# The mixer's products with h as seven block products, made ahead of the branch products, with the gates kept in DRAM

## The chip, the cores and the metric

The kernel runs on one NeuronCore of a Trainium2 chip. The metric is the device time of one execution in microseconds (us). The engines are TensorE (PE, with its weight loads listed as PEld), VectorE (DVE), ScalarE (ACT), GpSimd (POOL) and SyncE (SP), whose queue issues the DMAs. They run beside each other, each in the order of its own queue, and wait for each other by semaphores. [...]

## What is computed

One layer of a diffusion backbone over 512 latent and 128 context tokens (T = 640), model width 1024, all in float32. The mixer, which the change is about, stands between two SwiGLU blocks (FFN1, FFN2):

```python
z = h @ w_in
q, k, v, g, u, vs, gates = jnp.split(z, IN_SPLITS, axis=-1)
...
r = r.transpose(0, 2, 1, 3).reshape(B, L, RET_V) * g_ret
ret_out = (jax.nn.silu(g) * r) @ w_ret_br
u = jax.nn.gelu(u)
vsf = jax.nn.gelu(vs)
...
sp = jnp.einsum('gij,bnjgc->bnigc', w_sp, vsn) + b_sp.T[:, :, None]
sg_out = (u * sp.reshape(B, L, SG_WIDTH)) @ w_sg_br
gate_r, gate_s = jnp.split(jax.nn.sigmoid(gates), 2, axis=-1)
y = (gate_r * ret_out + gate_s * sg_out) @ w_out
```

In the parts left out, r is the retention per head in both directions, normed, and vsn is the LayerNorm of vsf with g_sg and b_sg. g, u and both gates are four products of the same h with 1024 x 1024 weights; the outputs keep float32 accuracy.

## The kernel before

A float32 matrix is held as two parts, a rounded one (hi) and the rest (lo), and each product is three passes: hi·hi, hi·lo, lo·hi. For h these are the tiles HH and HL, [128, 8, 640]: 8 slices k of 128 features, 640 tokens. Weights come as 512 KB blocks by DMA into `raw`, ACT rounds them to `whi` (L199), and DVE or POOL subtracts to get `wlo` (L206). One list, `steps`, sets in which order the weights are used; `stream` and `flow` prepare them ahead of PE (two steps with `take`, seven with `take7`), five pairs of buffers in a ring. The schedule is written by hand: the program's order is each engine's order.

The mixer runs in these parts. Six groups of token-major products (`group`, matmuls of 512 columns): 0 to 3 give q, k, v of a head each, 4 and 5 give vs, which ACT turns by gelu into VS (the tile F1). Beside them a queue of small tasks, `bg`, works off the heads' retention (`head_tasks`), one task behind every twentieth part of a group; at the end the heads' r stands in F0. Then eight products each of u, gs with sg, g, gr, rt (`one`: 8 k x 3 passes, 384 columns in part A and 256 in part B, 48 matmuls). u stands first, with the LayerNorm of VS beside it: five `ln_step`s for each half of the features, a subtract-and-scale (L1346) and a multiply (L1347) on DVE and an addition on POOL (L1348); then `sp_step` multiplies gelu(u) with the spatial product into Z (tiles ZH, ZL). gs is used at once as sigmoid in the evacuation of sg, the branch product of Z. g gives silu(g)·r, the next Z; gr goes into F0; rt, the branch product, is gated and added, and H takes the sum. Boundary 2 is w_out on H, two norms and the next h; then FFN2.

FFN2 has the form that the change brings to the mixer: `seven` (L781) computes two output blocks over 1024 features as a 2 x 2 block product with seven instead of eight block multiplications (Winograd's scheme). For that the right side needs four sums and differences of the blocks of h, the "forms" (`right_forms`, L654; th, tl in the profile), and each pair of weight blocks four more sums (L161), with seven hi and lo parts of 512 columns (whis, wlos). A block is 4 k x 3 passes of 320 columns, 12 matmuls. Three PSUM banks per pair, X, Y, Z, collect the blocks q0 to q6; X goes on being added to after ACT has copied its state out (p1 after q0, u2 after q2, u3 after q4), so q2, q4 and q5 wait for a copy.

`newton_rsqrt` (L281) makes the reciprocal roots of all norms: three rounds, in each of them two instructions per column of 128 tokens.

## Time and profile before

| | us |
|---|---|
| median of 3 runs (lowest, highest) | 1646.86 (1642.75, 1648.46) |
| the profiled execution | 1649.0 |
| its span in the profile | 1647.2 |
| mean granted clock in it | 0.979 |
| mixer's products, from the end of group 5 to w_out's first matmul | 751.8 to 1099.7 |

The span is the time from the first to the last instruction of one profiled execution. The profiled execution is one run among others; a sum made from its rows is one against its own time, and the runs' median lies 2.1 us lower. Busy time is no measure of what bounds a stage: an engine that is busy 60% of the span can be full in one stage and idle in the next.

### The profile page before, as it was taken

The page shows a single profiled execution, that of the slowest core. Times are in us where ns is not written, and L with a number is a line of the kernel's source. Part 1 is how long each engine was busy: PE and PEld are TensorE (multiplying, and loading weights), DVE is VectorE, ACT ScalarE, POOL GpSimd, SP SyncE. Part 2 cuts the span into 40 slices and gives each one's busy share as a digit, 9 for nine tenths or more (in the row PEclk, how much of TensorE's full clock was granted, in tenths as well). Part 3 has the DMA queues.
Part 4 walks back from the last instruction along what each step waited for, and adds up shares of the span by engine and source line. Part 5 has one row for each costly group of instructions (what it writes and reads, how often), then busy time and mean ns, then how long its engine had stood idle before and what let it go on. Part 6 is the DMA issues. An engine that isn't in the chain of part 4 may idle for free. (4 is left out here: it accounts for less than half of the span.)

```text
span 1647.2 us, 25640 instructions
## 1 busy us (share of the span) xinstructions
PE 1587.5 (96%) x10294; PEld 1540.4 (94%) x10294; DVE 984.7 (60%) x1911; ACT 580.7 (35%) x1083; POOL 489.3 (30%) x304
## 2 busy tenths in 40 slices
PE   8899999999998999999999999999898999999995
PEld 8899999999998788889999999999897999999995
DVE  6768577776757866657621131235848656565656
ACT  4535212222223532332321233224445525344343
POOL 3322112221125322234211111114425434333334
PEclk9899999999998999999999999999899999999997
DMA  9035344443442322212222222233302223122231
GB/s 379 14 122 188 127 146 158 145 171 137 154 141 63 104 65 69 72 58 90 77 102 68 62 77 77 70 133 93 109 27 96 80 75 107 58 81 87 80 116 64
DMA packets 62599, 170.63 MB, mean 104 GB/s; under 512 B 5904, under 2 KB 22544, under 8 KB 62480
## 3 DMA queue, kind: packets, MB, share of 16 engines
q1 hardware_dynamic: 62336, 168.92, 30.7%
q8 instruction: 81, 1.33, 0.3%
q14 instruction: 38, 0.31, 0.1%
q10 hardware_dynamic: 144, 0.07, 0.0%
HBM read 160.05 MB, written 8.91 MB: 103 GB/s over the span
## 5 line engine op out<-in xcount | busy, mean ns | idle before, releaser
L206 POOL TENSOR_TENSOR wlo<-raw,whi 128x1024 fp32r<-128x1024 f32 (+2 forms) x90 | 222.5, 2473 | 754.8 <-ACT whi L199 718.3
L199 ACT CAST whi<-raw 128x1024 fp32r<-128x1024 f32 (+2 forms) x159 | 155.4, 997 | 73.2 <-DMA raw<-in_wout_dram 31.3
L206 POOL TENSOR_TENSOR wlos<-raw,whis 128x512 fp32r<-128x512 f32 (+1 forms) x61 | 83.5, 1371 | 165.3 <-ACT whis L199 133.5
L206 DVE TENSOR_TENSOR wlo<-raw,whi 128x1024 fp32r<-128x1024 f32 (+2 forms) x69 | 90.2, 1308 | 63.4 <-ACT whi L199 62.0
L308 PE MATMUL pBf<-HL,whi 128*128 128x256 f32 x416 | 117.7, 283 | 0.0
L309 PE MATMUL pBf<-HH,wlo 128*128 128x256 f32 x416 | 117.6, 283 | 0.0
L307 PE MATMUL pBf<-HH,whi 128*128 128x256 f32 x416 | 117.6, 283 | 0.0
L416 DVE CUSTOM_DVE_ANT_0 junkc<-wa,cb 128x1024 bf16<-128x1024 f32 x56 | 102.6, 1832 | 1.9
L314 PE MATMUL pg<-whi,HH 128*128 128x512 f32 x240 | 99.4, 414 | 0.0
L199 ACT CAST whis<-raw 128x512 fp32r<-128x512 f32 (+1 forms) x138 | 80.9, 604 | 50.4 <-PE pof213B L309 5.9
L315 PE MATMUL pg<-whi,HL 128*128 128x512 f32 x240 | 95.0, 396 | 0.3 <-DVE HL L384 0.3
L316 PE MATMUL pg<-wlo,HH 128*128 128x512 f32 x240 | 94.4, 393 | 0.0
L308 PEld LDWEIGHTS pBf<-HL,whi 128*128 128x128 f32 x416 | 79.6, 191 | 0.2 <-DVE HL L384 0.2
L309 PEld LDWEIGHTS pBf<-HH,wlo 128*128 128x128 f32 x416 | 79.6, 191 | 0.0
L307 PEld LDWEIGHTS pBf<-HH,whi 128*128 128x128 f32 x416 | 79.5, 191 | 0.0
L411 DVE CUSTOM_DVE_ANT_0 junk<-wa,cb 128x1024 bf16<-128x1024 f32 x58 | 77.1, 1329 | 2.8 <-DMA wa<-in_wada_dram 2.2
L206 DVE TENSOR_TENSOR wlos<-raw,whis 128x512 fp32r<-128x512 f32 (+1 forms) x77 | 66.9, 875 | 9.2 <-ACT whis L199 9.1
L795 PE MATMUL Xf<-th,whis 128*128 128x320 f32 x216 | 67.7, 314 | 2.9 <-ACT p1f L805 1.8
L797 PE MATMUL Xf<-th,wlos 128*128 128x320 f32 x216 | 67.2, 311 | 0.0
L796 PE MATMUL Xf<-tl,whis 128*128 128x320 f32 x216 | 67.2, 311 | 0.0
L316 PEld LDWEIGHTS pg<-wlo,HH 128*128 128x128 f32 x240 | 45.5, 190 | 10.3
L315 PEld LDWEIGHTS pg<-whi,HL 128*128 128x128 f32 x240 | 45.7, 190 | 8.4 <-DVE HL L384 0.6
(2712 smaller groups left out, 5218.5 us busy)
## 6 DMA issues: line engine op xcount, KB each, us to landing
raw<-in_win_dram SPq DMA_DIRECT2D x86, 512.0 KB, 4.4
wa<-in_wada_dram SPq DMA_DIRECT2D x60, 512.0 KB, 3.8
raw<-in_wmix_dram SPq DMA_DIRECT2D x56, 512.0 KB, 3.5
raw<-in_wgrp_dram SPq DMA_DIRECT2D x24, 512.0 KB, 3.6
raw<-in_wout_dram SPq DMA_DIRECT2D x32, 256.0 KB, 2.7
raw<-in_wout_dram SPq DMA_DIRECT2D x16, 384.0 KB, 4.1
st<-in_wada_dram SPq DMA_DIRECT2D x10, 512.0 KB, 10.5
raw<-in_wout_dram SPq DMA_DIRECT2D x16, 320.0 KB, 3.9
```

The lines of the kernel that those rows point to most:

```text
L199: A.copy(hi, parts_[i])
L206: eng.tensor_tensor(lo, parts_.pop(i), r32(hi), op=ALU.subtract)
L307: PE.matmul(ps, lhsT=whi[:, wc, :], rhs=hh[:, k, c0:c1], start=first, stop=False)
L308: PE.matmul(ps, lhsT=whi[:, wc, :], rhs=hl[:, k, c0:c1], start=False, stop=False)
L309: PE.matmul(ps, lhsT=wlo[:, wc, :], rhs=hh[:, k, c0:c1], start=False, stop=last)
L314: PE.matmul(ps, lhsT=HH[:, k, tk], rhs=whi[:, k % 2, :], start=k == 0, stop=False)
L315: PE.matmul(ps, lhsT=HL[:, k, tk], rhs=whi[:, k % 2, :], start=False, stop=False)
L316: PE.matmul(ps, lhsT=HH[:, k, tk], rhs=wlo[:, k % 2, :], start=False, stop=k == KT - 1)
L411: V.tensor_tensor_reduce(out=jk, in0=adas[t], in1=cb[:, 0, :], scale=1.0, scalar=0.0, op0=ALU.mult, op1=ALU.add, accum_out=mods[:, 0, ADA[ ...
L416: V.tensor_tensor_reduce(out=jk, in0=adas[t], in1=cb[:, 1, :], scale=1.0, scalar=0.0, op0=ALU.mult, op1=ALU.add, accum_out=mods[:, 1, ADA[ ...
L795: PE.matmul(ps, lhsT=whi[:, k, :], rhs=hi, start=first and k == 0, stop=False, skip_group_check=True)
L796: PE.matmul(ps, lhsT=whi[:, k, :], rhs=lo, start=False, stop=False, skip_group_check=True)
```

## The change

The products g, u, gs and gr of the mixer are made as seven block products, in pairs of output blocks, all but gr6 and gr7, which stay plain. All of them come before the branch products sg and rt. The order is: gr6, gr7 (plain), g (four pairs), u (four), gs (four), gr (three), sg, rt. The forms of h are made during group 5 and gr6, gr7 from the task queue. Since sg and rt come later than their gates, the sigmoids of gs and gr go to a DRAM scratch `gscr` by SP's queue and come back by it in the sg and rt loops (`reload`). silu(g)·g_ret·r is formed in F0, gelu(u) times the spatial product in F1 (VS); both are split into hi and lo later, into Z during the last seven and into H during sg. LayerNorm's two halves stand in the first and the third pair of g. rt's sum goes to Z instead of H, and w_out reads that.

With it: `newton_rsqrt` works on all columns at once, three instructions a round; half of the forms' lo parts go from DVE to POOL, in FFN2 too; each head has one pause less; buffers of the tail lie in two larger tiles (R2, R3), which hold the forms, then Z, then FFN2's hidden part and forms; two of w_out's weight blocks lie in HH and HL.

```diff
@@ the order of the weights
-    for i in range(56):
-        plain(wmix[i], KT * P, P, "wx" if i >= 48 + RING else None)
+    for i in (38, 39):
+        plain(wmix[i], KT * P, P)
+    for j in range(0, 16, 2):
+        i = 24 + j if j < 8 else j - 8
+        seven(wmix[i], wmix[i + 1])
+    for i in range(0, KT, 2):
+        seven(wmix[9 + 2 * i], wmix[11 + 2 * i])
+    for i in range(0, KT - 2, 2):
+        seven(wmix[32 + i], wmix[33 + i])
...
@@ newton_rsqrt
-            for b in range(n):
-                c = slice(b, b + 1)
-                V.scalar_tensor_tensor(t[:, c], y[:, c], y[:, c], v[:, c], op0=ALU.mult, op1=ALU.mult)
...
+            V.tensor_tensor(t, y, y, op=ALU.mult)
+            V.tensor_tensor(t, t, v, op=ALU.mult)
+            V.scalar_tensor_tensor(dst if it == 2 else y, t, 1.5, y, op0=ALU.add, op1=ALU.mult)
@@ right_forms
-                    late.append(lambda: eng.tensor_tensor(tl[n][:, k, :], t[to], r32(th[n][:, k, :]), op=ALU.subtract))
+                    late.append(lambda: (G if n in (1, 2) else V).tensor_tensor(tl[n][:, k, :], t[to], r32(th[n][:, k, :]), op=ALU.subtract))
...
+    def pair7(name, forms, out):
...
+        def keep(x):
+            t[x] = ntmp(nrm, HT, f"{x}{name}")
+            A.copy(t[x], X[0])
+        def plus(x, ps):
+            V.tensor_tensor(t[x], t[x], ps, op=ALU.add)
+            return t[x]
...
+        def q3():
+            prod(3, Yb, "Y", True)
+            out.c11(plus("p1", Yb[0]))
+        def q4():
+            prod(4, X, "X", False)
+            keep("u3")
+            out.c22(plus("u3", Z[0]))
+        def q5():
+            prod(5, X, "X", False)
+            out.c21(X[0])
+        def q6():
+            prod(6, Z, "Z", False)
+            out.c12(plus("u2", Z[0]))
...
+    group(4, vs_evac(0))
+    purge()
+    state["hfree"], state["eng"] = False, G
+    bg.append(close_heads)
+    group(5, vs_evac(1))
...
+    def sevens(items):
+        for name, out in items:
+            q = pair7(name, forms, out)
+            q[0]()
+            bgrun()
+            for f in held:
+                f()
+                bgrun()
+            for f in q[1:5]:
+                f()
+                bgrun()
+            held[:] = q[5:]
...
+    class Ret(Gate):
+        def then(self, m, h, d):
+            V.scalar_tensor_tensor(F0[:, m, h], F0[:, m, h], gret_s[:, m:m + 1], d, op0=ALU.mult, op1=ALU.mult)
+    class Stored(Gate):
...
+        def then(self, m, h, d):
+            bg.append(lambda: SP.dma_start(gscr[self.i, m, :, h], d))
...
+        bg.append(ln_stats)
+        bg.extend(ln_step(0, c) for c in range(NCK))
+        bg.extend([pause] * 4 + [lambda: (load_gb(2), load_gb(3))] + [pause] * 3)
+        bg.extend(ln_step(1, c) for c in range(NCK))
+        sevens([(f"g{m}", Ret(m, AF.Silu)) for m in range(0, KT, 2)])
+        sevens([(f"u{m}", Gelu(m)) for m in range(0, KT, 2)])
+        sevens([(f"gs{m}", Stored(m, 0)) for m in range(0, KT, 2)])
...
+        for m in range(KT):
+            s1 = one(take7(), Z, f"sg{m}")
+            for i, part in enumerate("AB"):
+                c0, c1 = COLS[part]
+                V.tensor_tensor(F1[:, m, c0:c1], gates[0, m][:, c0:c1], s1[i], op=ALU.mult)
+            split(H, m, chunks(F0[:, m, :]))
+            reload(0, m + 2)
```

Three places of the queues, as the programs have them. PE, the seam between two products: before, the last three matmuls of u0's part B and the first three of u1.

```order
L307 MATMUL u0B<-HH,whi_7158 128x256
L308 MATMUL u0B<-HL,whi_7158 128x256
L309 MATMUL u0B<-HH,wlo_7159 128x256
L307 MATMUL u1A<-HH,whi_7198 128x384
L308 MATMUL u1A<-HL,whi_7198 128x384
L309 MATMUL u1A<-HH,wlo_7199 128x384
```

After, the seam between q0 of the second g pair (bank Xg_7590) and q5 of the first (Xg_7462), which was held back behind it. Two products of 48 matmuls have become seven blocks of 12, on the forms (R) or on HH, HL.

```order
L733 MATMUL Xg_7590<-HH,whis_7374 128x320
L734 MATMUL Xg_7590<-HL,whis_7374 128x320
L735 MATMUL Xg_7590<-HH,wlos_7375 128x320
L733 MATMUL Xg_7462<-R_7124,whis_7292 128x320
L734 MATMUL Xg_7462<-R_7125,whis_7292 128x320
L735 MATMUL Xg_7462<-R_7124,wlos_7293 128x320
```

DVE at the LayerNorm: before, the last step of the second half's fourth chunk and the spatial step of u0 behind it (F_91 is VS, gu is gelu(u)).

```order
L1346 TENSOR_SCALAR F_91<-F_91,vmv,vrs 128x512
L1347 TENSOR_TENSOR F_91<-F_91,gb_7373 128x512
L1384 TENSOR_TENSOR spt0A<-sp0A,bsp_s 128x384
L1386 TENSOR_TENSOR gu_7355<-gu_7355,spt0A 128x384
L1384 TENSOR_TENSOR spt0B<-sp0B,bsp_s 128x256
L1386 TENSOR_TENSOR gu_7355<-gu_7355,spt0B 128x256
L1361 TENSOR_TENSOR ZL<-gu_7355,ZH 128x640
```

After, in the first g pair: the low part of the next pair's block, an ln step, then the addition that completes p1 (block q3) and silu(g)·r of it in F_84, which is F0, then the next ln step's first half and so on.

```order
L222 TENSOR_TENSOR wlos_7459<-s_111_7456,whis_7458 128x512
L1484 TENSOR_SCALAR F_88<-F_88,vmv,vrs 128x512
L1485 TENSOR_TENSOR F_88<-F_88,gb_7446 128x512
L742 TENSOR_TENSOR p1g_7475<-p1g_7475,Yg_7539 128x320
L1450 SCALAR_TENSOR_TENSOR F_84<-F_84,small,p1g_7475 128x320
L1484 TENSOR_SCALAR F_88<-F_88,vmv,vrs 128x512
```

The ln steps, which stood between plain products that ask nothing of DVE before their end, now stand among additions that PE's banks wait for.

ACT in the same place: before, weight casts, two gelus a product.

```order
L199 CAST whi_7379<-raw_7196 128x1024
L1392 ACTIVATE gu_7433<-u1A 128x384
L1393 ACTIVATE gu_7433<-u1B 128x256
L199 CAST whi_7444<-raw_7299 128x1024
L1392 ACTIVATE gu_7498<-u2A 128x384
L1393 ACTIVATE gu_7498<-u2B 128x256
L1360 CAST ZH<-gu_7355 128x640
```

After, between the first and the second g pair: a cast, the copy of p1 of the second pair, the silu of the first pair's c21, the silu of its u2 (from DVE's addition), three casts for the third pair, and the copy of u2 of the second pair (from Xg_7590), which PE needs before it adds q4 to that bank.

```order
L215 CAST whis_7559<-raw_7149 128x512
L739 COPY p1g_7603<-Xg_7590 128x320
L1433 ACTIVATE vationFunctionType.Silu_7624<-Xg_7462 128x320
L215 CAST whis_7627<-raw_7452 128x512
L1433 ACTIVATE u2g_7532<-u2g_7532 128x320
L215 CAST whis_7627<-s_117_7583 128x512
L215 CAST whis_7646<-s_118_7585 128x512
L215 CAST whis_7646<-raw_7452 128x512
L739 COPY u2g_7679<-Xg_7590 128x320
```

What moved: a copy out of PSUM that PE waits for now stands behind activations and casts that wait for DVE.

## Rows read from the trace of the kernel before

**Rows 1.** Part 1 of the page: busy time of each engine in us, its share of the span, and its instructions.

```profile
PE 1587.5 (96%) x10294; PEld 1540.4 (94%) x10294; DVE 984.7 (60%) x1911; ACT 580.7 (35%) x1083; POOL 489.3 (30%) x304
```

**Rows 2.** The table of stretches: stretch and its length in us, then the busy us (and instructions) of PE, of its weight loads, of DVE, ACT and POOL, then the mean granted clock of TensorE, the DMA engines' share and GB/s. The first two are the mixer's products, the third FFN2's forms, the last FFN2's seven-products.

```profile
753.00:828.00 75.00, 74.96 (x528) 74.56 (x526) 57.75 (x104) 21.78 (x35) 29.08 (x15) 1.00 0.24 77
828.00:1100.00 272.00, 271.59 (x1856) 271.40 (x1856) 64.36 (x83) 71.32 (x104) 45.61 (x19) 1.00 0.23 73
1240.00:1280.00 40.00, 33.30 (x207) 31.41 (x206) 35.14 (x54) 21.48 (x50) 20.52 (x16) 0.96 0.24 79
1272.00:1276.00 4.00, 4.00 (x18) 4.00 (x18) 2.71 (x5) 2.08 (x4) 1.77 (x2) 0.57 0.40 122
1280.00:1600.00 320.00, 317.87 (x2146) 315.08 (x2145) 196.36 (x320) 134.73 (x274) 120.34 (x86) 1.00 0.27 85
```

**Rows 3.** What PE waited for, from the list of waits: the group that waited, the engine and group that ended the wait, us in total, times, the longest.

```profile
PE adaps L362 <- DVE rsx0B L296: 2.4, 1, 2.4
PE csn3yB L362 <- DVE rsn3yB L296: 2.0, 1, 2.0
PE csn5yB L362 <- DVE rsn5yB L296: 2.0, 1, 2.0
PE sg0A L308 <- DVE ZL L1361: 0.4, 1, 0.4
```

**Rows 4.** ACT in order of time: start and duration in us, engine, line, operation, what is written from what, and in brackets the idle time before it and what ended that. First the last two gelus of group 5, then the first silu of two products of h that follow each other.

```profile
750.46 0.60 ACT L1312 ACTIVATE F<-pg 128x512 f32<-128x512 f32 x1 [0.76 <-PE pg L316]
751.82 0.60 ACT L1312 ACTIVATE F<-pg 128x512 f32<-128x512 f32 x1 [0.76 <-PE pg L316]
...
941.78 0.49 ACT L1414 ACTIVATE tg<-g1A 128x384 f32<-128x384 f32 x1 [1.15 <-PE g1A L309]
948.81 0.49 ACT L1414 ACTIVATE tg<-g2A 128x384 f32<-128x384 f32 x1 [1.15 <-PE g2A L309]
```

**Rows 5.** PE in order of time, same columns: the first of the spatial matmuls and the first of the next product; then the first of the last triple (one k) of block Yf and of the last triple of block Xf after it in FFN2, 12 matmuls apart.

```profile
772.74 0.83 PE L1382 MATMUL sp0A<-wsp_s,F 128*128 128x128 f32 x6
773.78 0.42 PE L307 MATMUL u3A<-HH,whi 128*128 128x384 f32 x1
...
1354.39 0.31 PE L795 MATMUL Yf<-HH,whis 128*128 128x320 f32 x1
1356.15 0.31 PE L795 MATMUL Xf<-th,whis 128*128 128x320 f32 x1
```

**Rows 6.** DVE in order of time while FFN2's forms are made: the first difference, two sums beside POOL, the last low part.

```profile
1241.90 0.48 DVE L678 TENSOR_TENSOR b<-b,b 128x320 f32<-128x320 f32 x1
...
1263.29 2.66 DVE L669 TENSOR_TENSOR b<-HH,HL 128x320 f32<-128x320 f32 x2
...
1270.74 1.56 DVE L682 TENSOR_TENSOR tl<-b,th 128x320 fp32r<-128x320 f32 x1
```

**Rows 7.** The table of stretches for two pairs of FFN2 (columns of rows 2).

```profile
1353.08:1377.72 24.64, 24.64 (x171) 24.64 (x170) 16.52 (x25) 11.82 (x25) 10.33 (x8) 1.00 0.21 66
```

**Rows 8.** DVE in order of time in the LayerNorm of vs (L1346, L1347) and the first spatial step (L1384, L1386).

```profile
760.49 0.54 DVE L1346 TENSOR_SCALAR F<-F,vmv,vrs 128x512 f32<-128x512 f32 x1
761.06 1.67 DVE L1347 TENSOR_TENSOR F<-F,gb 128x512 f32<-128x512 f32 x1
762.65 0.54 DVE L1346 TENSOR_SCALAR F<-F,vmv,vrs 128x512 f32<-128x512 f32 x1
...
773.16 0.55 DVE L1346 TENSOR_SCALAR F<-F,vmv,vrs 128x512 f32<-128x512 f32 x1
...
774.34 0.54 DVE L1346 TENSOR_SCALAR F<-F,vmv,vrs 128x512 f32<-128x512 f32 x1
...
776.72 0.55 DVE L1384 TENSOR_TENSOR spt0A<-sp0A,bsp_s 128x384 f32<-128x384 f32 x1
...
778.74 1.08 DVE L1386 TENSOR_TENSOR gu<-gu,spt0B 128x256 f32<-128x256 f32 x1
```

**Rows 9.** DMA issues by line: destination and source, queue, operation, count, KB each, median us from issue to landing.

```profile
out_dram<-ns SPq DMA_DIRECT2D x8, 128.0 KB, 1.7
gb<-in_gsg_dram SPq DMA_DIRECT2D x2, 256.0 KB, 4.8
```

**Rows 10.** Groups of ACT's instructions in FFN2's seven-products, 1300 to 1500: line, engine, operation, names, shapes, count, busy us and mean ns of one, idle before.

```profile
L199 ACT CAST whis<-raw 128x512 fp32r<-128x512 f32 x66 | 39.6, 617 | 36.7 <-PE pof213B L309 5.9 <-PE pof223B L309 5.9 <-PE pof215B L309 5.8
L818 ACT ACTIVATE s1f<-s1f 128x320 f32<-128x320 f32 x10 | 4.7, 472 | 10.5 <-DVE s1f L817 10.5
```

**Rows 11.** DVE in order of time, the reciprocal root of two norms of the last stage: a round over three columns and the start of the next, then two chained instructions, a round over two columns, and the start of the next.

```profile
1617.62 0.48 DVE L293 SCALAR_TENSOR_TENSOR ntn5yA<-nyn5yA,nvn5yA 128x1 f32<-128x1 f32 x3
1618.23 0.48 DVE L293 SCALAR_TENSOR_TENSOR ntn5yA<-nyn5yA,nvn5yA 128x1 f32<-128x1 f32 x3
...
1635.93 0.17 DVE L288 TENSOR_SCALAR nyn5yB<-nvn5yB 128x2 int32<-128x2 int32 x1
1636.14 0.17 DVE L289 TENSOR_SCALAR nvn5yB<-nvn5yB 128x2 f32<-128x2 f32 x1
1636.34 0.35 DVE L293 SCALAR_TENSOR_TENSOR ntn5yB<-nyn5yB,nvn5yB 128x1 f32<-128x1 f32 x2
1636.81 0.35 DVE L293 SCALAR_TENSOR_TENSOR ntn5yB<-nyn5yB,nvn5yB 128x1 f32<-128x1 f32 x2
```

**Rows 12.** POOL in order of time, the addition of the same ln step.

```profile
760.65 1.53 POOL L1348 TENSOR_TENSOR F<-F,gb 128x512 f32<-128x512 f32 x1 [4.83 <-DVE F L1347]
```

More of the change, by code (lines that the diff above doesn't have):

```diff
@@ L96, in hybrid_kernel @@
             plain(wgrp[g, u], KT * P, 512)
-    for i in range(56):
-        plain(wmix[i], KT * P, P, "wx" if i >= 48 + RING else None)
+    for i in (38, 39):
[7 more added lines that the diff above has]
+        seven(wmix[32 + i], wmix[33 + i])
+    for i in [8 + 2 * m for m in range(KT)] + list(range(40, 56)):
+        where = None
+        if i >= 48 + RING:
+            where = "wx" if i == 48 + RING else i - 51
+        if i == 50:
+            stop2 = len(steps)
+        plain(wmix[i], KT * P, P, where)
     ahead2 = len(steps) + NAHEAD
@@ new lines, in hybrid_kernel, with group @@
+    ahead = {1: (wts[g0[4]], pg1)}
+    rate = {"n": 1}
+    def group(g, evac):
+        w0, pgs = ahead.pop(g, (None, {}))
+        done = len(pgs)
+        pgs = pgs | {c: psum(f"pg{g}{c}") for c in range(done, NCK)}
+        i = 0
+        for u in range(4):
+            w = w0 if u == 0 and w0 else take7() if g == 5 else take(eng=V if g == 1 and u < 2 else G)
+            for c in range(done if u == 0 else 0, NCK):
+                for k in (2 * u, 2 * u + 1):
+                    tok_mm(pgs[c], w, k, c)
+                if u == 3:
+                    evac(c, pgs[c])
+                i += 1
+                bgrun(rate["n"])
@@ new lines, in hybrid_kernel, with vs_evac, go @@
+    for h in range(NH):
+        vs, move = head_evac(h)
+        if h == 0:
+            b1.lead["E"] = lambda c: move(c, pg0[c])
+            b1.run(B1B)
+        else:
+            group(h, move)
+        bg.extend(head_tasks(h, vs))
+    VS = F1.rearrange("p k t -> p (k t)").rearrange("p (c f) -> p c f", c=NCK)
+    def vs_evac(j):
+        def go(c, ps):
+            o = VS[:, c, j * 512:(j + 1) * 512]
+            A.activation(o, ps, AF.Gelu_apprx_tanh)
+            V.bn_stats(vst[:, c, j, :], o)
+        return go
```

613 lines of the change are left out of this document (315 added, 298 removed).

## The prediction

> **What bounds the kernel now.** Read first the page's busy shares [rows 1]: TensorE (PE) is busy 96% of a span of 1647.2 us, VectorE (DVE) 60%, ScalarE (ACT) 35%, GpSimd (POOL) 30%. Then the table of stretches [rows 2], since an average hides stages. In the two stretches from 753 to 1100 us, which are the mixer's products, PE is busy 346.55 of 347 us at a granted clock of 1.00; so a matmul less is time less there, and nothing else is. In the first of them, though (753 to 828, where the LayerNorm of vs and the gating run), DVE is busy 57.75 of 75 us, while in the 272 us after it has 64. From 1240 to 1280 PE loses 6.7 of 40 us: there FFN2 makes its "forms", the same helper that the change now runs in the mixer too. Last, the list of what PE waited for [rows 3]: its long waits lie at the norms between the stages; the mixer's longest is 0.4 us. The chain of waits is no help: it covers only the last 30 us.
>
> **The PE work that goes.** One product of h (1024 rows, 128 outputs, 640 columns) comes every 7.03 us (941.78 to 948.81) [rows 4]. Two of them are 14.06 us, 96 matmuls. FFN2 already works by seven block products: one block is 12 matmuls of 320 columns, 1354.39 to 1356.15, that is 1.76 us [rows 5], so a pair of outputs costs 7 x 1.76 = 12.32 us. Fifteen pairs change over (g, u, gs four each, gr three; gr6 and gr7 stay plain): 15 x 1.74 = **26.1 us less**. The order agrees: 9829 PE rows become 9649, 180 fewer, 15 x 12. All other PE work stays. This is the only gain; the rest is what it costs.
>
> **The forms of h, 0 us (0 to 4).** They now run beside group 5 and gr6, gr7. Group 5's last matmul ends at 751.8, where its last gelu starts [rows 4]; q0 of the first pair can start at 751.8 + 14.06 = 765.9, q1, which needs the first form whole, at 767.6. The head tasks end some 4 us earlier than now (three pauses fewer in the heads before, 1.36 us of PE each, by the gelus' distance), so DVE is free at about 732 to 734. Its part: 8 sums, 15 differences, 7 low parts at 0.4 us start to start, 5 statistics and 6 weight steps at about 0.6 us, that is 19 us, and to this what POOL's work adds: FFN2's forms took DVE from 1241.9 to 1272.3 [rows 6], 30 us with similar weight steps; 734 + 30 = 764, before 767.6. Hidden, with 4 us to spare; POOL has eight low parts more than in FFN2, which may eat these.
>
> **LayerNorm in the first pair, +5.5 us (1 to 11).** This work moves from beside plain products to beside seven-products, which load DVE far more: two pairs of FFN2 hold DVE for 16.5 of 24.6 us [rows 7], 8.2 each, and a pair of g has as many DVE instructions of the same size. One ln step now takes 2.16 us start to start (760.49 to 762.65) [rows 8], so five add 10.8 to the 8.2, and before them stand the statistics' small instructions, 12 x 0.2 us. They stand in DVE's queue ahead of the addition p1 (the DVE rows of the change). DVE reaches the first ln step at 764 + 7.4 = 771.4 or a little later; its multiplier cannot be there before, as its load stands on SP behind the store of gr7's gate: 766.3 + 4.8 [rows 9] = 771. After a multiply, a weight step and another ln step p1's addition starts between 774 and 779; its block q3 ends at 765.9 + 4 x 1.76 = 772.9. Behind it in ACT's queue stand silu (0.47 [rows 10]) and the copy of u3, without which q5 may not add to the same bank; q5 is due at 776.4. So PE waits 0 to 4 us. Then DVE has three more ln steps and five weight steps, 8 us bare and 13 at the rate of rows 8, before the addition of u2; in ACT's queue its silu and two or three casts (0.62 each) stand ahead of the next pair's copy of u2, which q4 of that pair needs (the ACT rows of the change). Due at 785 to 789, it comes at 787 to 795: 1 to 7 us. Both ends kept; 5.5 taken, the middle: in rows 8 the steps ran at the slow rate from 760 on and at 1.18 us a step (773.16 to 774.34) once POOL waited for its load.
>
> **The second half of LayerNorm, in the third pair, +2.5 us (0 to 7).** Three ln steps before p1's addition put it 4 us late with 2.5 us of slack: 1.5; the copy of u2 then comes about 2 late if the slow rate holds, nothing if not.
>
> **The u pairs, +1 us (0 to 6).** DVE's 8.2 us less four gating steps (0.45 each) plus two spatial steps of at most 3.1 (776.72 to 779.8 [rows 8]): 12.6 us of a pitch of 12.32 + 2 x 1.04 (the sp matmuls, 772.74 to 773.78 [rows 5]). Just below, so little is lost.
>
> **Clock after such stalls, +1.5 us (0 to 4).** [...]
>
> **Gates through DRAM, the end of the sevens, +0.5 us (0 to 4).** 32 stores of 128 to 192 KB and 16 loads of 320. A store of 128 KB lands in 1.7 us [rows 9]. The buffer of p1 is wanted again by c21 three blocks (5.3 us) later, of which the addition, the sigmoid and the store take about 3.5. The next weights stand on SP behind a store that waits for a sigmoid, but they are needed ten blocks later. Z's splits go into the last seven's blocks; the last two need ACT and DVE for some 3 us, while sg0 reaches k = 7 after 5.4 us.
>
> **newton_rsqrt, +1.4 us (0.4 to 2.7).** Three chained instructions a round instead of two per column. Chained ones stand 0.2 us apart (1635.93, 1636.14) [rows 11]: nine are 1.8 us. A round over two columns takes 0.47 (1636.34 to 1636.81), three rounds 1.4; over three columns 0.61 (1617.62 to 1618.23), three rounds 1.8. So +0.4 us at each two-column norm that PE waits for: rsx0B, rsn3yB and rsn5yB in rows 3, and half of it at one more. [...]
>
> **FFN2's forms, 0 us (-3 to +4).** Eight low parts move from DVE (0.4 us each, 3.2) to POOL. But in rows 6 DVE's own instructions stretch when POOL works (two sums 2.66 instead of 0.8), so they come back. The rest of the diff around FFN2 (buffers, names) leaves the order of boundary 2 as it is.
>
> **Sum.** -26.1 + 5.5 + 2.5 + 1.0 + 1.5 + 0.5 + 1.4 = -13.7 us. The profiled run took 1649.0 us (1647.2 of it span), the median of the runs is 1646.9, so 2.1 lower: **1633 us**.
>
> **The rivals.** *The cover holds, 1624 us.* DVE's queue runs ahead by the seven blocks that the flow prepares, and the ln steps take 1.18 us instead of 2.16; then the stalls stay at 4 us: -26.1 + 4 + 1.4 = -20.7, and a little off for FFN2. For it: FFN2's pairs keep PE busy 317.9 of 320 us [rows 2]. Against: they have no LayerNorm beside them.
> *DVE and POOL take strict turns, 1644 us.* At 761.06 DVE's multiply lasted 1.67 us while POOL's addition ran from 760.65 for 1.53 [rows 12]. If this holds for all of both halves of LayerNorm, take the upper ends, 11 + 7, with 1 for u, 2.5 of clock and 1.4: -26.1 + 22.9 = -3.2. [...]
> *Slower, 1659 us.* The same turns through all eight g and u pairs, so that DVE and POOL together set the pitch: POOL takes 10.3 us for two pairs, 5.2 each [rows 7]. u pairs 12.6 + 5.2 = 17.8 instead of 14.4, g pairs without ln 13.4 instead of 12.3, with the 18 above: 4 x 3.4 + 2 x 1.1 + 18 = 34 us, more than the 26.1 that go; with 3 of clock and 1.4, +12. It decides from 3.3 us a pair. Against it: in FFN2 both engines work beside each other (DVE 196, POOL 120 of 320 us [rows 2]) and PE does not wait.
> That the change does not do what it says is ruled out by the 180 rows.
>
> **Numbers.** Forecast 0.45 (own range 1627 to 1641), cover holds 0.28, strict turns 0.19, slower 0.08. Within 0.3% (1642 to 1652, about what a measurement here can tell from none) fall most of the strict turns and a sliver of the forecast: 0.14. Slower: 0.08 and a little of the turns, 0.09. Faster: 0.77. The range leaves out the last rival and the best tenth: 1620 to 1647.
>
> **What would show it.** Fifteen pairs 12.3 us apart where nothing waits: the first term. PE waits on ACT's copies (L739) in the first and third g pair, with DVE full there: the ln terms; none there: the cover. PE waits spread over all u pairs: the slower rival. rsn5yB 0.4 us later after its column sum: newton. PE waiting for weights or for DMA in gs and gr, or for a form at q1, would be a cause that I put at nothing, and wrong.

## The result and the profile after

The changed kernel takes 1663.74 us (median of 4 runs, 1663.24 to 1664.66), the kernel before 1647.01: a ratio of 1.0107, 95% interval 1.0087 to 1.0126. It is slower by 1.1%; 1633 was predicted, with 1620 to 1647 as the range. The profiled execution took 1664.07 us, 1662.0 of it span.

Page part 1 of the changed kernel, the row that answers to [rows 1]:

```profile
PE 1569.8 (94%) x10114; PEld 1518.2 (91%) x10114; DVE 1099.7 (66%) x1972; ACT 632.6 (38%) x1220; POOL 565.2 (34%) x374
```

PE has 180 instructions and 17.7 us of work less, DVE 115 us more. The table of stretches, which answers to [rows 2] (columns as there): the heads with the groups beside them, the two plain products, the four g pairs, the u and gs pairs, the gr pairs.

```profile
529.00:763.00 234.00, 222.25 (x1096) 185.04 (x1096) 160.47 (x432) 88.79 (x173) 81.22 (x56) 0.98 0.24 76
763.10:777.20 14.10, 14.10 (x98) 14.10 (x97) 10.79 (x15) 5.30 (x11) 6.90 (x7) 1.00 0.00 1
777.20:848.50 71.30, 55.07 (x314) 53.23 (x313) 62.94 (x94) 29.26 (x61) 41.67 (x28) 0.87 0.26 91
848.50:957.20 108.70, 108.70 (x754) 108.70 (x754) 79.65 (x117) 56.35 (x116) 44.60 (x34) 0.99 0.30 96
957.20:999.20 42.00, 40.75 (x277) 40.50 (x277) 21.90 (x31) 24.43 (x49) 19.30 (x12) 1.00 0.52 165
```

The plain products and the u and gs pairs are full. In the first stretch PE is idle for 12 of 234 us (2.5 before), in the g pairs for 16 of 71, at a granted clock of 0.87, where 1.00 is the highest that the traces show. The list of what PE waited for, which answers to [rows 3]:

```profile
PE rt L1310 <- DVE rn L1299: 9.0, 4, 3.5
PE Xg L733 <- ACT u2g L739: 6.4, 2, 3.5
PE Xg L733 <- ACT u3g L739: 6.1, 3, 3.2
PE Xg L733 <- ACT p1g L739: 2.5, 1, 2.5
...
PE adaps L383 <- DVE rsx0B L317: 2.5, 1, 2.5
PE csn3yB L383 <- DVE rsn3yB L317: 2.3, 1, 2.3
PE csn5yB L383 <- DVE rsn5yB L317: 2.3, 1, 2.3
```

The first four waits are new. `rt` is the transposition of a head's r, `rn` the normed r that it needs from DVE; the others are the copies L739 that free bank X in the g pairs. From the starts in PE's order of time (plain product: the first matmul behind group 5; w_out: the first matmul of its second block, 1103.35 and 1115.33 us), this is where the time went:

| stage | before | after | difference |
|---|---|---|---|
| to 529 us (norms of boundary 1) | 528.94 | 527.36 | -1.6 |
| heads, to the first plain product after group 5 | 222.68 | 235.73 | +13.0 |
| products, to w_out's second block | 351.73 | 352.24 | +0.5 |
| rest of w_out, FFN2, the last stage | 543.85 | 546.67 | +2.8 |
| span | 1647.2 | 1662.0 | +14.8 |

w_out's own first matmul stands at 1099.18 us before (the table ahead of the prediction has 1099.7) and at 1111.16 after, which gives the same differences. The first row's -1.6 is not the change's: that start came anywhere from 525.7 to 529.3 us in the runs below. The products should have lost 26.1 us of PE's work, so 26.6 are lost in them. The g pairs take 71.35 us from their first block to the first of u, where 26 blocks of 1.76 are 45.8: 25.6 us, all but one.

The blocks themselves are as forecast. PE in order of time in the gs pairs, the first matmuls of two blocks that follow each other (q1 and q2 of a pair):

```profile
925.43 0.31 PE L733 MATMUL Zgs<-R,whis 128*128 128x320 f32 x1
...
927.20 0.31 PE L733 MATMUL Xgs<-R,whis 128*128 128x320 f32 x1
```

They stand 1.76 us apart.

**The heads.** The last head of the changed kernel, in order of time (columns as in [rows 4]): POOL's low parts of three weights, the first small instructions of newton_rsqrt on DVE beside them; then one more low part, the last small instruction beside it, the normed r, and the transposition on PE with its wait.

```profile
725.39 7.08 POOL L222 TENSOR_TENSOR wlo<-raw,whi 128x1024 fp32r<-128x1024 f32 x3 [7.07 <-ACT whi L215]
...
727.43 0.39 DVE L311 TENSOR_SCALAR nvpv<-mv 128x2 f32<-128x2 f32 x1
727.85 2.28 DVE L312 TENSOR_SCALAR nypv<-nvpv 128x2 int32<-128x2 int32 x1
730.17 2.33 DVE L313 TENSOR_SCALAR nvpv<-nvpv 128x2 f32<-128x2 f32 x1
...
738.24 2.35 POOL L222 TENSOR_TENSOR wlo<-raw,whi 128x1024 fp32r<-128x1024 f32 x1 [5.76 <-ACT whi L215]
...
738.33 2.27 DVE L317 SCALAR_TENSOR_TENSOR rs<-ntpv,nypv 128x2 f32<-128x2 f32 x1
740.63 0.99 DVE L1299 TENSOR_SCALAR rn<-pv,mv,rs 128x256 f32<-128x256 f32 x2
...
741.68 1.11 PE L1310 MATMUL rt<-cst,rn 128*128 128x128 f32 x4 [3.04 <-DVE rn L1299]
```

An instruction on 128 x 2 numbers took 0.17 us with POOL idle [rows 11]. Beside POOL's subtractions of 2.4 us each it took 2.28 and 2.33 here, that is until the one beside it was over, and twice in a row, as POOL has three of them. So rn is late and PE waits 3.04 us. The kernel before has two such holds of full length in its heads, 2.33 and 2.26 us, and PE waits for neither: its heads have time enough. One of them, a first instruction of newton_rsqrt:

```profile
683.86 2.26 DVE L287 TENSOR_SCALAR nvpv<-mv 128x2 f32<-128x2 f32 x1
```

Of the 13.0 us in the heads 9.0 are these waits; most of the rest, 3.4 us, is low clock behind the two longest, 0.50 for some 3.4 us each (columns as in the table of stretches):

```profile
698.00:700.00 2.00, 2.00 (x6) 1.52 (x5) 2.00 (x7) 0.37 (x1) 0.00 (x0) 0.50 0.54 205
742.00:744.00 2.00, 2.00 (x8) 1.71 (x7) 1.67 (x11) 0.59 (x1) 0.00 (x0) 0.50 0.79 324
```

**A g pair.** The same view in the first g pair: on POOL the addition of one ln step and a weight sum; beside them on DVE the next ln step, and the addition of p1 behind it; on ACT a weight cast, a table load, the silu of p1 and the copy of u3; and the matmul on PE that waits for the copy.

```profile
789.80 1.67 POOL L1486 TENSOR_TENSOR F<-F,gb 128x512 f32<-128x512 f32 x1 [7.33 <-DVE F L1485]
791.43 1.48 POOL L177 TENSOR_TENSOR raw<-raw,raw 128x512 f32<-128x512 f32 x1
...
790.23 1.52 DVE L1484 TENSOR_SCALAR F<-F,vmv,vrs 128x512 f32<-128x512 f32 x1
791.78 1.67 DVE L1485 TENSOR_TENSOR F<-F,gb 128x512 f32<-128x512 f32 x1
793.38 0.47 DVE L742 TENSOR_TENSOR p1g<-p1g,Yg 128x320 f32<-128x320 f32 x1
...
792.94 0.62 ACT L215 CAST whis<-raw 128x512 fp32r<-128x512 f32 x1 [5.09 <-POOL raw L177]
793.58 1.28 ACT L1433 ACT_TABLE_LOAD   x1
794.87 0.47 ACT L1433 ACTIVATE p1g<-p1g 128x320 f32<-128x320 f32 x1
...
795.76 0.42 ACT L739 COPY u3g<-Xg 128x320 f32<-128x320 f32 x1
...
796.23 0.56 PE L733 MATMUL Xg<-R,whis 128*128 128x320 f32 x1 [2.56 <-ACT u3g L739]
```

The ln step takes 3.2 us (790.23 to 793.38) in place of 1.2, its two instructions ending 0.3 and 0.5 us behind POOL's two. p1's addition runs at once then, but on ACT its silu stands behind a cast that waits for POOL's sum, and behind a table load; the copy stands behind the silu. DVE is busy for 63.0 of the 71.35 us of the g pairs, and of its 8 idle ones it spends 5.8 waiting for such silus: the two engines wait for each other. Dips of the clock follow, two stretches of the changed kernel (columns as above):

```profile
810.00:814.00 4.00, 3.71 (x16) 3.71 (x17) 4.00 (x4) 0.76 (x2) 3.37 (x3) 0.57 0.36 137
832.00:836.00 4.00, 4.00 (x16) 4.00 (x16) 3.43 (x6) 0.47 (x1) 2.91 (x3) 0.50 0.00 0
```

Within 1.4 us of the end of each of the five waits of 2.5 us and more in the g pairs the granted clock falls from 1.00 to 0.50, once for 6.8 us and four times for some 3.4 (0.57 and 0.50 are the means of these two stretches), and PE's matmuls of 320 columns come every 0.27 us in place of 0.15. So of the 25.6 us in the g pairs 16.2 are waits; the other 9.4 are nearly all low clock, as 18 us at 0.50 lie in the g pairs, half of which is 9.0.

### The profile page after: what moved, and what is told of

It is laid out like the page before. It is cut to its first block, busy times and chain, and to the rows that moved or that the text cites. A ratio compares the mean times of both kernels' runs of the same rounds, so it can differ in the third digit from the quotient of the medians.

```text
span 1662.0 us, 25762 instructions
## 1 busy us (share of the span) xinstructions
PE 1569.8 (94%) x10114; PEld 1518.2 (91%) x10114; DVE 1099.7 (66%) x1972; ACT 632.6 (38%) x1220; POOL 565.2 (34%) x374
## 5 line engine op out<-in xcount | busy, mean ns | idle before, releaser
L222 POOL TENSOR_TENSOR wlo<-raw,whi 128x1024 fp32r<-128x1024 f32 (+2 forms) x73 | 183.6, 2517 | 577.3 <-ACT whi L215 565.2
L222 POOL TENSOR_TENSOR wlos<-raw,whis 128x512 fp32r<-128x512 f32 (+1 forms) x90 | 126.6, 1410 | 241.0 <-ACT whis L215 205.8
L215 ACT CAST whi<-raw 128x1024 fp32r<-128x1024 f32 (+2 forms) x127 | 122.3, 984 | 104.9 <-issue 32.7
L215 ACT CAST whis<-raw 128x512 fp32r<-128x512 f32 (+1 forms) x213 | 126.2, 608 | 81.5 <-POOL raw L177 15.3
L222 DVE TENSOR_TENSOR wlos<-raw,whis 128x512 fp32r<-128x512 f32 (+1 forms) x123 | 103.1, 848 | 11.6 <-ACT whis L215 11.4
L733 PE MATMUL Xf<-TH,whis 128*128 128x320 f32 x216 | 66.9, 310 | 5.8 <-ACT p1f L739 3.0
L177 POOL TENSOR_TENSOR raw<-raw,raw 128x512 f32<-128x512 f32 x33 | 48.2, 1462 | 69.3 <-DVE s L177 63.6
L734 PE MATMUL Xf<-R,whis 128*128 128x320 f32 x216 | 66.7, 309 | 0.0
L735 PE MATMUL Xf<-TH,wlos 128*128 128x320 f32 x216 | 66.3, 307 | 0.0
L222 DVE TENSOR_TENSOR wlos<-s,whis 128x512 fp32r<-128x512 f32 x66 | 53.7, 834 | 6.3 <-ACT whis L215 6.1
```

Source lines behind the costliest of these rows:

```text
L215: A.copy(hi, parts_[i])
L222: eng.tensor_tensor(lo, parts_.pop(i), r32(hi), op=ALU.subtract)
L733: PE.matmul(ps, lhsT=whi[:, k, :], rhs=hi, start=first and k == 0, stop=False, skip_group_check=True)
L734: PE.matmul(ps, lhsT=whi[:, k, :], rhs=lo, start=False, stop=False, skip_group_check=True)
```

## The experiments

All times are medians, ratios are to the kernel before, run beside. The kernel before, run anew beside each set of experiments, came out between 1645.9 and 1648.3, so 2 us between sets are not told apart by the time alone; stages are compared by the starts in the traces.

### The ln steps

Without them, so that this kernel leaves out LayerNorm's subtraction, scaling and addition:

```diff
-        bg.extend(ln_step(0, c) for c in range(NCK))
...
-        bg.extend(ln_step(1, c) for c in range(NCK))
```

> The ten ln steps of vs (subtract-and-scale, multiply, addition) are left out, the statistics and the loads stay. In the changed kernel the four g pairs take 71.4 us from the first q0 to the first q0 of u, where 26 blocks of 1.76 are 45.8: 25.6 us lost, 16.2 of it waits, the rest low clock. Theory LN (the steps stand ahead of the additions and copies that PE waits for): the waits in the second to fourth pair go (2.6, 3.5, 3.2, 3.0 us) and the low clock with them, so the g pairs take 48 to 53 us and the run is 18 to 22 us faster. Rival forms (the forms of h end 16 us later than planned and DVE never recovers): the waits stay in the first two pairs and less than 10 us comes back.

Measured 1645.65 us, 18.1 less than the changed kernel; ratio 0.9988 (0.9976 to 0.9999). The g pairs take 52.1 us:

```profile
778.30:830.40 52.10, 48.17 (x315) 47.38 (x314) 43.79 (x74) 29.53 (x62) 24.65 (x18) 0.97 0.37 124
```

So the ln steps cost 19 of the 25.6 us: 12.3 are waits (3.9 are left of 16.2), the other 7 low clock (a mean of 0.97 in place of 0.87). 6.3 us stay without them, in the first pair.

Their additions on DVE:

```diff
-                G.tensor_tensor(o, o, gb[2 * f + 1], op=ALU.add)
+                V.tensor_tensor(o, o, gb[2 * f + 1], op=ALU.add)
```

> The additions of the ln steps run on DVE and not on POOL. Theory port (a POOL instruction beside DVE holds DVE's instruction up until it ends): ten POOL additions of 1.3 to 1.7 us go, DVE gets ten of 0.6 to 0.7 and loses the stretches of its 0.54 us instructions to 1.5 us, so the g pairs get 3 to 8 us shorter. Rival load (DVE's own work ahead of the copies is what counts): 10 x 0.6 = 6 us more on DVE, the g pairs get 3 to 6 us longer.

Measured 1665.67 (1.0111, 1.0091 to 1.0132), the g pairs 73.5 us, 2 longer. Neither theory's number. The groups of DVE's instructions in the g pairs say why; first the changed kernel, then this one:

```profile
L1484 DVE TENSOR_SCALAR F<-F,vmv,vrs 128x512 f32<-128x512 f32 x10 | 11.2, 1123 | 0.0
...
L1485 DVE TENSOR_TENSOR F<-F,gb 128x512 f32<-128x512 f32 x10 | 8.9, 886 | 0.3
```

```profile
L1485 DVE TENSOR_TENSOR F<-F,gb 128x512 f32<-128x512 f32 x10 | 8.8, 884 | 0.3
L1486 DVE TENSOR_TENSOR F<-F,gb 128x512 f32<-128x512 f32 x10 | 7.9, 791 | 0.3
...
L1484 DVE TENSOR_SCALAR F<-F,vmv,vrs 128x512 f32<-128x512 f32 x10 | 5.4, 540 | 0.0
```

Without POOL's addition beside it the subtraction takes 0.540 in place of 1.123 us, ten times. That is theory port, POOL's instruction holding DVE's up, and 5.8 us; but the additions then cost DVE 7.9. In sum DVE's time for the steps goes from 20.1 to 22.1 us, and PE follows by just that.

The steps spread over the four g pairs:

```diff
-        bg.extend(ln_step(0, c) for c in range(NCK))
+        lnq.extend(ln_step(0, c) for c in range(NCK))
+        every["n"] = 2
...
+                every["i"] += 1
+                if lnq and every["i"] % every["n"] == 0:
+                    lnq.popleft()()
```

> The statistics, the ten ln steps and the loads between them stand behind every second block of the four g pairs, in place of five in a row, twice. Theory bunch (five steps in a row stand ahead of an addition that PE's bank needs): a step alone takes some 2.2 us and finds 2.5 us of slack, so the waits of 2.6 to 3.5 us go, the g pairs fall from 71.4 us to 55 to 60, the run gets 11 to 16 us faster. Rival total (DVE is full in the g pairs as a whole, some 88% busy from 777 to 850): the waits only move, g pairs 68 to 72 us, 0 to 4 us faster.

Measured 1663.89 (1.0100, 1.0080 to 1.0121): nothing. The first block of u comes after 66.1 us, but the g blocks held back behind it wait 3.1 us, and gs begins at 905.75 as in the changed kernel (905.59). The waits have only moved: the bunch theory falls.

The steps as two instructions on DVE and none on POOL:

```diff
-                V.tensor_scalar(o, o, vmv[:, c, 0:1], vrs[:, c:c + 1], op0=ALU.subtract, op1=ALU.mult)
-                V.tensor_tensor(o, o, gb[2 * f], op=ALU.mult)
-                G.tensor_tensor(o, o, gb[2 * f + 1], op=ALU.add)
+                V.scalar_tensor_tensor(o, o, vmv[:, c, 0:1], gb[2 * f], op0=ALU.subtract, op1=ALU.mult)
+                V.scalar_tensor_tensor(o, o, vrs[:, c:c + 1], gb[2 * f + 1], op0=ALU.mult, op1=ALU.add)
```

> The changed kernel, with each ln step as two DVE instructions with two operands and a scalar each, (x - m) * g and then * rs + b, in place of two on DVE and one on POOL; the bare time on DVE stays about 1.2 us a step, POOL's ten additions of 1.3 to 1.7 us go. In the g pairs DVE's instructions now take 19.8 us more than the same ones alone. Theory port: half of this goes, the g pairs fall from 71.4 to 62 to 66 us, 5 to 9 us faster. Rival load (DVE's own count of instructions ahead of the copies): the g pairs stay within 2 us.

Measured 1658.97 (1.0071, 1.0056 to 1.0086), 4.8 less; the g pairs 67.7 us, 3.6 less. DVE's time for the steps falls from 20.1 to 17.8 us, at the low end of what the theory said; POOL's other work still runs beside. PE's waits in the g pairs add up to 16.1 us as before. What went is low clock, at a mean granted clock of 0.92 in place of 0.87.

Three gs pairs ahead of g, the steps behind every fourth block of seven pairs:

```diff
+    for i in range(0, KT - 2, 2):
+        seven(wmix[9 + 2 * i], wmix[11 + 2 * i])
     for j in range(0, 16, 2):
...
-    for i in range(0, KT, 2):
+    for i in range(KT - 2, KT, 2):
```

> Three pairs of gs stand ahead of g, and the same steps stand behind every fourth block of seven pairs (gs0, gs2, gs4, g). Theory total: a pair has some 4 us of DVE to spare and now gets 1.6 steps of 2.2 us, so most of the 25.6 us lost in the g pairs goes: 14 to 19 us faster than the changed kernel, 1645 to 1650. Theory bunch: the same as with the steps behind every second block, within 3 us.

Measured 1658.34 (1.0070, 1.0049 to 1.0092), 5.4 less, where 14 to 19 were expected. The seven pairs lose 15.5 us (98.3, where 47 blocks are 82.8) in place of 25.6. Of the 10 us that they win, 4 are lost again behind them, between u's first block and w_out. So DVE's load in the g pairs is part of it, but pairs with DVE to spare wait too.

### The heads

The kernel before with the two parts of the change that touch the heads:

```diff
-                    s_pv((0, 1)), s_pv((2, 3)), s_pv((4,)), pause, s_rt((0, 1)), pause, s_rt((2, 3)), pause, s_rt((4,))]
+                    s_pv((0, 1)), s_pv((2, 3)), s_pv((4,)), pause, s_rt((0, 1)), pause, s_rt((2, 3)), s_rt((4,))]
...
-            for b in range(n):
...
+            V.tensor_tensor(t, y, y, op=ALU.mult)
+            V.tensor_tensor(t, t, v, op=ALU.mult)
+            V.scalar_tensor_tensor(dst if it == 2 else y, t, 1.5, y, op0=ALU.add, op1=ALU.mult)
```

> The kernel before, with two small parts of the change alone: the new newton_rsqrt and the head's pause taken out. If these two make the heads late, the transpositions wait for rn as in the changed kernel: 8 to 12 us slower than before. If it takes the weight steps that the change puts on POOL ahead of its block products as well: the waits of the last head stay away, 2 to 6 us slower.

Measured 1657.46 us (1.0064, 1.0046 to 1.0081), 10.4 more than the kernel before, with the same wait in its list, which stands nowhere in that of before:

```profile
PE rt L1265 <- DVE rn L1254: 6.6, 3, 3.5
```

The two alone bring the waits; block products are not needed for them. By the trace the heads lose 9.1 us here (231.8 for 222.7), against 13.0 in the changed kernel. The first two waits are the same in both, 1.7 and 3.5 us; the last head waits 1.3 us here and 3.8 there, where POOL makes all low parts beside it.

Each of them undone in the changed kernel, the pause and then newton_rsqrt:

> The pause ahead of each head's last transposition is back, 1.36 us of PE work each. The heads lose 12 us against the kernel before, 9.0 of it four waits of the transpositions for rn (1.69 and 3.52 ahead of a last one, 0.71 and 3.04 ahead of a first and a second). Rival pause (the pause alone was the slack): all four waits go, 9 to 12 us faster. Theory port (POOL's weight steps hold newton's small instructions for 2.3 us, wherever they fall): the waits at the last transpositions get 1.4 us shorter each, the others stay: 2 to 5 us faster.

> newton_rsqrt is that of the kernel before again. At the norms my step said 1.4 us back in all. In the heads its chains get 0.4, 0.4 and 0.6 us shorter. Theory port: the last transpositions wait 1.4 us less at most, the others stay, 1 to 4 us faster in all. Rival newton (its longer chain makes the heads late): three of the four waits go, 6 to 10 us faster.

The pause: 1662.98 (1.0095, 1.0075 to 1.0114), 0.8 less. The waits for rn fall from 9.0 to 2.8 us and the heads get 7.3 us shorter, but the g pairs 5.4 longer, with 5.1 us of waiting for a form of h. The old newton: 1658.28 (1.0072, 1.0053 to 1.0091), 5.5 less, the heads 8.7 us shorter, the g pairs 3.1 longer. The size in the heads came out within what rival newton expected, but not its way: five waits for rn stay, 4.6 us in all, none of them over 1.8, so the waits give 4.4 of the 8.7 us; that the rest is low clock that went, of which the changed kernel has 3.4 us in the heads behind its two longest waits, is an estimate. That the products give part of it back neither theory had.

Both together:

> The changed kernel with the pause and the old newton only; the ln steps stand as the change has them. If the heads' 12 us were a loss of their own: 10 to 12 us faster, 1652 to 1654. If DVE stays behind into the forms and the g pairs (each of the two alone gave back 3.1 and 5.4 us there): 4 to 8 us faster, 1656 to 1660, with longer waits for the forms and for u2 and u3 of the g pairs.

Measured 1654.80 (1.0053, 1.0036 to 1.0070), 8.9 less, between the two. From its list of waits, the last of them new:

```profile
PE Xg L736 <- ACT u3g L742: 7.7, 3, 4.4
PE Xg L736 <- ACT u2g L742: 6.2, 2, 3.4
PE Zg L736 <- ACT R L702: 4.8, 1, 4.8
```

The heads are 13.1 us shorter, as before the change, and the g pairs lose 5.7 more.

POOL's low parts in group 5:

```diff
-    state["hfree"], state["eng"] = False, G
+    state["hfree"] = False
```

> The changed kernel, but the low parts of the plain weights used in group 5, gr6 and gr7 alternate between DVE and POOL as in the kernel before; in the change POOL makes them all, 2.4 us each. Theory port (each of them holds newton's small DVE instructions up: 2.28, 2.33 and 2.27 us in the last head): half of the holds go, DVE gets 1.3 us for each, the transpositions' waits fall from 9.0 to 4 to 6 us and the run is 2 to 5 us faster. Rival (pause and newton alone, which cost the kernel before 10.4 us): nothing in it, within 1.5 us.

Measured 1665.26 (1.0101, 1.0086 to 1.0116): nothing. The heads get 2.4 us shorter, all in the last head (its waits fall from 3.8 to 2.5 us), and the g pairs 2.2 longer; PE's waits there are 16.8 us, 0.6 more than before, so by difference most of this would be low clock, which is an estimate. Why is not shown.

### What is left, and a version that is faster

Steps over seven pairs, pause and old newton together; then the two-instruction steps on top; then the low parts of the edit above as well:

> As the run before, and the heads get their pause back and newton_rsqrt its old form. If the heads' 12 us and the g pairs' 25.6 are two losses of their own: 8 to 12 us faster again, 1634 to 1641. If both are one DVE that is behind from the third head on (the pause alone gave back 5.4 of its 6.4 us in the g pairs, the old newton 3.1 of 8.4): the forms come late for q1 and 3 to 6 us are left, 1641 to 1646.

> The kernel with the steps spread over seven pairs, the pause and the old newton (1648.9 us), with the ln step as two DVE instructions and none on POOL. Theory port: 3 to 6 us faster than that, 1643 to 1646. Rival load: within 2 us of it, 1647 to 1651.

> As the run before, and the low parts of the plain weights in group 5, gr6 and gr7 alternate between DVE and POOL again. The forms of h are late for q1 by 4.9 us with pause and old newton. Theory port: POOL's holds on DVE go and the forms end earlier, 1 to 4 us faster. Rival load: DVE gets 1.3 us for each that POOL gave up and the forms end later, 0 to 3 us slower.

Measured 1648.91 (1.0017, 1.0005 to 1.0029), 1645.86 (0.9990, 0.9977 to 1.0003) and 1645.83 (0.9987, 0.9978 to 0.9997): 9.4 less than with the spreading alone, 3.0 less again (the low end of what theory port said), then nothing. The 9.4 lie within what two losses of their own would give, yet the heads are 13.9 us shorter and the seven pairs 5.3 longer: here too part was given back, with 4.9 us of waiting for a form. The last one's list of waits has the forms in front:

```profile
PE Zgs L738 <- ACT R L704: 4.6, 1, 4.6
```

Activations behind the copies, in the changed kernel:

```diff
         def keep(x):
             t[x] = ntmp(nrm, HT, f"{x}{name}")
             A.copy(t[x], X[0])
+            while later:
+                later.popleft()()
...
-            out.c11(plus("p1", Yb[0]))
+            s = plus("p1", Yb[0])
+            defer(lambda: out.c11(s))
...
-            out.c12(plus("u2", Z[0]))
+            s = plus("u2", Z[0])
+            defer(lambda: out.c12(s))
```

> The changed kernel, with one thing moved in ACT's queue: the activation of a block that needs DVE's addition (p1, u2) is issued behind the next copy that PE waits for (u3, the next pair's u2), not ahead of it. No work is added or taken away. Theory queue (ACT stands at an activation that waits for DVE, and the copy behind it with it): the waits for u3 (6.1 us) and u2 (6.4 us) in the g pairs fall to less than 4 together and the low clock after them too; g pairs 56 to 62 us in place of 71.4, 9 to 15 us faster. Rival (DVE is full in the g pairs and PE waits for it by another way, the banks and the low parts of the weights): the waits take other names, less than 4 us faster.

Measured 1664.24 (1.0103, 1.0086 to 1.0120): nothing, and the waits have taken another name:

```profile
PE Zg L734 <- DVE u3g L745: 10.3, 4, 3.3
...
PE Xg L734 <- ACT u3g L740: 3.2, 2, 2.3
```

Most copies come in time now, and PE waits nearly as long (15.6 us in the g pairs for 16.2), one block later, for DVE itself: q6 may not add to bank Z before DVE has added it to u3. The stretch of the g pairs:

```profile
778.85:846.59 67.74, 52.17 (x315) 50.16 (x314) 64.00 (x90) 30.31 (x61) 42.09 (x28) 0.92 0.29 94
```

It is 3.6 us shorter than in the changed kernel, by less low clock (0.92 in place of 0.87), and DVE, which waits for silus for 1.6 us in place of 5.8, is busy 64.0 of 67.7 us; the profiled run loses as much elsewhere. So in the changed kernel ACT's order is worth 3.6 us of the 25.6 at most; DVE is late by either way. Two loads of ACT's tables of 1.28 us each, in the first pair, stand in the same chain; no run took them out.

The same in the kernel with 1645.83; four plain products ahead of the pairs in it, with the steps behind every third block of the six pairs that are left; and both:

```diff
-    for i in (38, 39):
+    for i in (38, 39, 21, 23):
...
-    for m in range(KT - 2, KT):
-        g1 = one(take7(), H, f"gr{m}", lambda: bgrun(4))
+    for r, m in ((1, KT - 2), (1, KT - 1), (0, KT - 2), (0, KT - 1)):
+        g1 = one(take7(), H, f"gr{r}{m}", lambda: bgrun(4))
```

> The same move in the kernel with the ln steps spread, two DVE instructions a step, the pause, the old newton and the low parts alternating (1645.8 us). What is left there in the first seven pairs is 19 us: some 9.6 at the first pair's forms, the rest waits for u3 and u2. Theory queue: the second part goes, 5 to 8 us faster, 1638 to 1641. Rival (DVE full): within 3 us.

> The kernel with 1645.8 us, with gs6 and gs7 as plain products behind gr6 and gr7, so that the forms of h have 14 us more until the first block needs one; this gives up one pair's 1.74 us. Theory forms (they end some 8 us too late): the first pair's waits of 4.6, 0.8, 1.5 and 1.6 us and the low clock go, 9.6 us, so 5 to 8 us faster, 1638 to 1641. Rival (DVE is full, what the forms let go the ln steps take): 0 to 3 us faster.

> Both moves. If the forms' lateness and ACT's queue are two causes: 10 to 15 us faster than 1645.8, 1631 to 1636, and faster than the kernel before by 0.7% or more. If both are one full DVE: 1640 to 1645.

Measured 1642.79 (0.9973, 0.9963 to 0.9983), 1638.60 (0.9945, 0.9931 to 0.9960) and 1633.46 (0.9917, 0.9902 to 0.9931). The plain pair, which costs 1.74 us of PE, brings 7.2: so the forms of h had cost some 9 us. The order of ACT brings 3.0 without the plain pair, at the rival's bound, and 5.1 with it: once DVE is late by little, the copies that pass it count. Both together are faster than the kernel before by 0.83%. Its six pairs ahead of u (70.4 us of blocks), and what PE still waits for there:

```profile
778.20:857.50 79.30, 73.46 (x483) 72.03 (x482) 76.37 (x123) 38.61 (x80) 34.90 (x24) 0.98 0.36 122
```

```profile
PE Zg L739 <- DVE u3g L750: 5.4, 3, 2.2
```

DVE is busy 76 of 79 us, and PE still waits for it: it is what bounds this stage.

Last, FFN2's low parts on DVE again:

```diff
-  late.append(lambda: (G if n in (1, 2) else V).tensor_tensor(tl[n][:, k, :], t[to], r32(th[n][:, k, :]), op=ALU.subtract))
+  late.append(lambda: (G if n in (1, 2) and tag == "h" else V).tensor_tensor(tl[n][:, k, :], t[to], r32(th[n][:, k, :]), op=ALU.subtract))
```

> The fastest so far (1633.5 us), with the low parts of FFN2's forms all on DVE again, as in the kernel before. From w_out's end to the first block of FFN2 the changed kernel loses some 2.6 us against the one before, this one some 2. If the eight low parts on POOL are the cause: 1 to 3 us faster. If it is the weight steps that now stand elsewhere in that stage: within 1 us, or slower by up to 3 as DVE gets 3.2 us more.

Measured 1631.45 (0.9910, 0.9894 to 0.9926). The total is not told apart from 1633.46, but from w_out's second block to a product late in FFN2 (pof232B) it takes 365.0 us in place of 367.6 (before the change 367.3, in the changed kernel 368.8), and the wait at FFN2's first pair, 3.0 us in the changed kernel, is that of the kernel before again:

```profile
PE Xf L739 <- ACT p1f L745: 1.8, 1, 1.8
```

## Why the prediction was wrong

**The PE work, -26.1 us: right.** 180 matmuls (10294 and 10114 in the traces; the prediction's 9829 and 9649 stand in no view, their difference is the same), 1.76 us a block, 12.3 a pair wherever nothing waits.

**The heads: the step that failed first.** The prediction took the removed pauses for a gain: "The head tasks end some 4 us earlier than now". It looked at what the pause delays and not at what it covers. Between a head's last matmul on v and its last transposition DVE has three chains of newton to run; in the kernel before they end just in time (its list shows no wait for rn, and in the third head rn is done 0.15 us before the last transposition starts). newton_rsqrt was priced at the norms only, +1.4 us, where it cost some 0.7 (the waits for rsx0B, rsn3yB and rsn5yB are 0.1, 0.3 and 0.3 us longer); its rounds take 0.4 us more as predicted (599.07 to 600.82 in the first head, 1.75 us where it was 1.37), but the whole call only 0.25 (2.24 for 1.99). The twelve calls in the heads were not in the sum at all. The heads lost 13.0 us where the sum has nothing; the two alone, in the kernel before, lost 9.1 there.

**The forms, 0 (0 to 4): too short, and late by what came ahead of them.** They were to take DVE from 734 to 764, 30 us as in FFN2. First and last DVE instruction in the changed kernel, then in the run with the pause and the old newton:

```profile
744.87 0.48 DVE L689 TENSOR_TENSOR b11h<-HH,HL 128x320 f32<-128x320 f32 x1
...
783.54 0.48 DVE L702 TENSOR_TENSOR R<-b21h,R 128x320 fp32r<-128x320 f32 x1
```

```profile
736.95 0.48 DVE L692 TENSOR_TENSOR b11h<-HH,HL 128x320 f32<-128x320 f32 x1
...
775.13 0.49 DVE L705 TENSOR_TENSOR R<-b21h,R 128x320 fp32r<-128x320 f32 x1 [0.52 <-ACT R L702]
```

They take 39 us in both, so the heads made them begin late and did not make them long. In the changed kernel DVE stands idle for some 9 of the 39, 4.1 of it for ACT's casts of weights and 2.5 for the gelus of vs; how much POOL's eight low parts add is not shown. PE's waits at the first pair, 2.5 and 1.1 us, are for ACT, where a copy of p1 and the sigmoids of gr6 stand behind a cast that waits 3.4 us for a form. They are as short as this because the heads had already held PE up: with the heads mended 7 us of waits appear (4.8, 0.8 and 1.5), and the plain pair showed some 9 in all.

**LayerNorm, +5.5 and +2.5: right in place, and in their ranges; the clock, +1.5: far too small.** PE's waits stand where the working put them: at u3's copy in the first and the third pair and at u2's in the pairs behind these. The first half's are 2.6 and 3.5 us, with 0.3 at u3 of the second pair, 6.3 where 5.5 (1 to 11) was taken; the second half's 3.2 and 3.0, 6.2 where 2.5 (0 to 7) was. No run shows the clock's term of 1.5 (0 to 4), which was the author's estimate. What the traces show: in the kernel before 4 us at a mean clock of 0.57 behind FFN2's waits [rows 2], 1.7 us by 0.43 x 4; in the changed kernel five falls to 0.50 at the five waits in the g pairs, most of 9.4 us. Together the ln steps cost 19 us by the run without them. What would have warned is a sum over the stage, since each wait was worked out from the slack at its place: from rows that stood there DVE has 4 x 8.2 us for the pairs, ten steps of 2.16 and 2.4 for the statistics, 57 us, in four pairs of 12.32, 49. A local slack does not help an engine with so much to do: spreading the steps brought nothing and passing ACT's queue 3.6 us at most; leaving the steps out brought 19 us in the g pairs, and giving DVE seven pairs for them 10.

**Strict turns, given 0.19: the hold is there, its price is smaller.** In the traces DVE's instruction outlasts POOL's: at the place of [rows 12] it ends at 762.73 us where POOL's ends at 762.18, and in the last head those of 0.17 us take 2.28 and 2.33. The upper ends of the two ln terms, 18 us, are about what the steps cost, but with 7 us of low clock in it; the waits are 12.5. The price is not POOL's whole time, though: taking the ten additions away brought 4.8 us of their 15.7.

**The slower rival, 1659 us: near the number, wrong in place, so the nearness is luck.** It put the loss in all g and u pairs. The u and gs pairs lose 2 us in 108.7; the terms of u (+1) and of the gates (+0.5; 42.0 us for 40.5 of blocks in gr) were within their ranges.

**FFN2's forms, 0 (-3 to +4): within the range.** The changed kernel takes 1.5 us more than the kernel before from w_out's second block to late in FFN2. Moving the low parts back to DVE brought 2.5 there in the fastest version, so POOL's making them did not come out as DVE's relief.

The sum by what was measured: -1.6 + 13.0 + 0.5 + 2.8 = +14.8 us (by unrounded terms), where -13.7 was predicted. Pause and newton together, undone, give the heads' 13.1 us back; which part each of them and of POOL's holds has cannot be given: they add to one lateness, and each one undone gave part back further on. That POOL's holds make the 3 us waits in the heads was read from the trace; the run that moved half of POOL's low parts away shortened the heads by 2.4 us only.
